# A modulation's columns: row sums of transposed weights on Vector in place of products on TensorE

## The chip, the core and the metric
One core of a Trainium2 chip runs one layer of a latent diffusion backbone. The metric is the time of one execution on the device in microseconds (us): the median of 3 runs, beside one execution that the hardware profiler recorded. The engines are PE (TensorE, matrix products), PEld (its weight loads), DVE (Vector), ACT (Scalar), POOL (GpSimd) and SP (SyncE, whose queue issues nearly all DMA transfers here).

## What is computed
One conditioning vector c gives six vectors of 2048 columns each: shift, scale and gate of the attention half, and shift, scale and gate of the feed-forward.

```python
mod = silu(c) @ ada_w + ada_b                      # ada_w: 2048 x 12288
sh1, sc1, g1, sh2, sc2, g2 = split(mod, 6)
z = modulate(rmsnorm(x, norm1_g), sh1, sc1) @ w_in # also for the context, with c_ctx
attn = windowed_gqa(...)                           # 16 heads, 4 kv heads, 512 tokens, 256 context tokens
rw = rwkv_output(...)                              # 16 heads of RWKV-7, both directions
x = x + g1 * (concatenate([attn, rw]) @ w_out)
x = x + g2 * swiglu(modulate(rmsnorm(x, norm2_g), sh2, sc2), w1, w3, w2)
return rmsnorm(x, final_norm_g)
```

There are 512 latent tokens, 256 context tokens, a width of 2048 and a feed-forward of 5632. All is float32. The last four of the six vectors are needed for the latents alone (the context isn't carried on after this layer), so they are one matrix-vector product with 8192 columns: 64 MB of weights, each used once.

## The kernel before
Channels lie on the 128 partitions and tokens along the row. Large products are made of three products of float32r parts (`mm3`, L109 to L114: high by high, low by high, high by low). A weight tile, 128x1024, is loaded into the ring `raw` (`split_weight`, L96 to L106, three buffers), Scalar copies its high part `whi` (L105) and Vector subtracts to get the low part `wlo` (L106). Of z = h @ w_in a column tile needs two such weights.

`modT` holds the modulation by columns of 128: 0 to 15 sh1, 16 to 31 sc1, 32 to 47 g1, 48 to 63 sh2, 64 to 79 sc2, 80 to 95 g2. `ada_group` (L146 to L171) computes 512 columns, that is four of these: eight loads of 512 KB (L154), 16 products 32x512 of silu(c) by the weights (L155, `ps_ada`), a copy to SBUF on Scalar (L164, `adas`), four small products that turn the row into columns (L167, `ps_adat`) and an addition of the bias on Vector (L168). Groups 0 to 7, sh1 and sc1, come at the start, before norm 1 can be finished. Groups 8 to 23 come as `ada_stream` (L1090) in the recurrence: its first loads wait for a load of w_out (`gate`), and its products are pinned where the program writes them.

The program then has these stages:
- **Start, keys and values**, to about 240 us: norms, the first groups of the modulation, the first column tiles of z. For the values four weights are split, and narrow products follow each.
- **Attention**, 240 to about 525 us. There are 32 units (2 groups by 4 blocks of queries by 4 pairs of heads). Of each: scores on TensorE, the row's maximum on Vector (L445), a few small steps (L447 to L449), Scalar's exponentials with their sum (L452), 1/sum and the scaling on Vector (L454 to L457), then transposes on TensorE (L466), their copy on Scalar (L467) and, every four units, the product by the values. Only TensorE's order is written by hand (`manual_schedule`): the scores of unit u + 2 go between the transposes of unit u, and shares of a stream of column tiles of z between both. The order of the other engines comes from a scheduler that simulates a timeline.
- **Preparation of the recurrence**, to about 1000 us.
- **Recurrence**, to about 1865 us: eight head pairs, each in three stretches of chunks, as streams `front`, inverse and chain (L860, L822, L967 and others). Behind each step's products `fill` lets other streams go on: `out_stream` (partial products of w_out, L110 to L114 under the name `ps_op`), `ada_stream` and `gate_stream`. How far each should be is a table, `DUE`. At the end of a pair stands `finish` with its output products (L994, `ps_y`).
- **Step to the feed-forward**: the last row tile of the recurrence's output is split (L1020, L1021, `alo`), the products with the last two row tiles of w_out go into the banks that are free, and `add_rows` (L1182) adds `g1` times them to x on Vector.
- **Feed-forward**, from about 1920 us: weights split as above (L1228 to L1231), 4 groups of 11 column tiles, `ps_u` and then `ps_d`, with `g2` at L1278.

Vector and SyncE execute in order: what waits holds back all that stands behind it on its engine.

## Time and profile before
| | |
|---|---|
| three runs | 3396.3, 3404.6, 3408.9 us; median 3404.6 |
| profiled execution | span 3398.9 us, 50708 instructions |
| busy share | PE 95%, DVE 49%, ACT 34%, POOL 17% |
| moved | 448 MB, 132 GB/s on the mean |

The profiled execution is one run of its own; its span is 5.7 us below the median of the runs. Busy time is the time in which an engine executes something. A wait is an engine's idle time just before an instruction, put down to what ended it. PEclk is the clock that TensorE was granted, as a share of its full speed of 2.4 GHz.

### The profile page before, as it was taken

The numbers are of one execution on the slowest core, as the hardware profiler recorded it, in microseconds if no ns is written. First come the engines' busy times: TensorE is split into PE (matmuls) and PEld (weight loads), VectorE is DVE, ScalarE is ACT, GpSimd is POOL, SyncE is SP. The second block draws the span as 40 slices with busy tenths as digits, with TensorE's granted clock in tenths as the row PEclk, the third lists the DMA queues.
The fourth block names the chain that finished last, engine by engine and source line by source line (L and its number), as shares of the span: only waits on it lengthen the run. The fifth ranks groups of instructions, "written<-read, shape, count | busy, mean of one in ns | idle before, by whom it ended". The sixth has DMA issues, their size and how long they took to land.

```text
span 3398.9 us, 50708 instructions
## 1 busy us (share of the span) xinstructions
PE 3238.6 (95%) x20448; PEld 2481.5 (73%) x20448; DVE 1652.3 (49%) x2674; ACT 1169.2 (34%) x2019; POOL 592.5 (17%) x613
## 2 busy tenths in 40 slices
PE   7899999889889999999998899999999999999997
PEld 3486667767665766777776688888888888888886
DVE  3345544786675666668876632332333332332333
ACT  4224443443434444445544422212221222212221
POOL 0000001563464423434442200000000000000011
PEclk9999999999989999999999899999999999999998
DMA  8611112333348789855557122322232223322232
GB/s 305 245 64 49 45 39 69 136 131 125 109 154 258 238 262 278 253 173 155 149 155 223 42 97 94 106 86 93 93 103 94 89 94 100 102 86 96 93 103 89
DMA packets 246858, 448.45 MB, mean 132 GB/s; under 512 B 84320, under 2 KB 131680, under 8 KB 246624
## 3 DMA queue, kind: packets, MB, share of 16 engines
q1 hardware_dynamic: 246624, 445.22, 40.6%
q8 instruction: 161, 2.64, 0.3%
q14 instruction: 73, 0.60, 0.1%
HBM read 383.52 MB, written 61.60 MB: 131 GB/s over the span
## 4 chain that ended last, share of the span: by engine, by line
PE 56%; DVE 3%; DMA 2%; ACT 1%; issue 1%; POOL 0%; SPq 0%; ACTq 0%; DVEq 0%; POOLq 0%
PE ps_u L114 10%; PE ps_u L113 10%; PE ps_u L110 9%; PE ps_d L110 5%; PE ps_d L114 5%; PE ps_d L113 5%; PE ps_m L941 2%; PE ps_y L822 1%; PE ps_op L110 1%; PE ps_i L860 1%; PE ps_x L811 1%; PE ps_w L930 1%; PE ps_op L113 1%; PE ps_op L114 1%; PE ps_ada L155 1%; PE ps_i L866 1%
## 5 line engine op out<-in xcount | busy, mean ns | idle before, releaser
L1230 ACT ACTIVATE whi<-raw 128x1024 fp32r<-128x1024 f32 (+1 forms) x240 | 275.1, 1147 | 1115.2 <-PE ps_u L113 585.6
L1231 DVE TENSOR_TENSOR wlo<-raw,whi 128x1024 fp32r<-128x1024 f32 (+1 forms) x238 | 317.8, 1336 | 557.3 <-ACT whi L1230 556.6
L114 PE MATMUL ps_u<-ahi,wlo 128*128 128x512 f32 x1408 | 560.8, 398 | 1.2 <-DVE wlo L1231 1.2
L113 PE MATMUL ps_u<-alo,whi 128*128 128x512 f32 x1408 | 557.9, 396 | 0.9 <-DVE alo L1246 0.9
L110 PE MATMUL ps_u<-ahi,whi 128*128 128x512 f32 x1408 | 553.3, 394 | 3.3 <-ACT ahi L1241 1.7
L110 PEld LDWEIGHTS ps_u<-ahi,whi 128*128 128x128 f32 x1408 | 265.1, 188 | 68.9 <-ACT whi L1230 2.9
L113 PEld LDWEIGHTS ps_u<-alo,whi 128*128 128x128 f32 x1408 | 265.2, 188 | 68.7 <-DVE alo L1246 1.6
L114 PEld LDWEIGHTS ps_u<-ahi,wlo 128*128 128x128 f32 x1408 | 265.1, 188 | 63.5 <-DVE wlo L1231 2.0
L198 POOL TENSOR_TENSOR sq<-sq 128x512 f32<-128x512 f32 x22 | 39.8, 1808 | 1429.4 <-ACT sq L194 1429.2
L113 PE MATMUL ps_d<-glo,whi 128*128 128x512 f32 x704 | 273.3, 389 | 0.0
L110 PE MATMUL ps_d<-ghi,whi 128*128 128x512 f32 x704 | 273.3, 389 | 0.0
L114 PE MATMUL ps_d<-ghi,wlo 128*128 128x512 f32 x704 | 273.3, 389 | 0.0
L114 PE MATMUL ps_z<-hhi,wlo 128*128 128x512 f32 x544 | 221.1, 406 | 38.9 <-DVE wlo L106 38.9
L110 PE MATMUL ps_z<-hhi,whi 128*128 128x512 f32 x544 | 228.1, 419 | 2.5 <-DVE wad L278 1.3
L113 PE MATMUL ps_z<-lo,whi 128*128 128x512 f32 x544 | 220.2, 405 | 0.0
L1278 DVE SCALAR_TENSOR_TENSOR x<-ps_d,modT,x 128x512 f32<-128x512 f32 x64 | 48.1, 751 | 299.8 <-PE ps_d L114 299.8
L852 POOL TENSOR_TENSOR bdB<-XY,mk 64x256 f16<-64x256 f32 x192 | 146.6, 764 | 266.0 <-DVE XY L813 248.2
L106 DVE TENSOR_TENSOR wlo<-raw,whi 128x1024 fp32r<-128x1024 f32 x80 | 123.0, 1544 | 137.7 <-ACT whi L105 134.5
L114 PEld LDWEIGHTS ps_z<-hhi,wlo 128*128 128x128 f32 x544 | 106.1, 195 | 69.6 <-DVE wlo L106 46.3
L155 PE MATMUL ps_ada<-ada,siluT 128*32 128x512 f32 x768 | 137.6, 612 | 18.1 <-DMA ada<-ada_w 14.1
L114 PEld LDWEIGHTS ps_d<-ghi,wlo 128*128 128x128 f32 x704 | 132.2, 188 | 27.5
L110 PEld LDWEIGHTS ps_d<-ghi,whi 128*128 128x128 f32 x704 | 132.2, 188 | 27.4
(617 smaller groups left out, 5824.3 us busy)
## 6 DMA issues: line engine op xcount, KB each, us to landing
ada<-ada_w SPq DMA_DIRECT2D x192, 512.0 KB, 6.0
raw<-w SPq DMA_DIRECT2D x176, 512.0 KB, 3.2
raw<-w SPq DMA_DIRECT2D x64, 704.0 KB, 4.1
raw<-w_in SPq DMA_DIRECT2D x72, 512.0 KB, 3.3
p1d<-pr SPq DMA_DIRECT2D x64, 256.0 KB, 3.2
bkd<-bk SPq DMA_DIRECT2D x16, 768.0 KB, 5.4
XB<-bkd SPq DMA_DIRECT2D x96, 128.0 KB, 3.9
pr<-p1d SPq DMA_DIRECT2D x48, 256.0 KB, 3.1
```

What stands on the lines that cost most here:

```text
L106: nc.vector.tensor_tensor(lo, raw, hi.bitcast(F32), op=ALU.subtract)
L110: mm = nc.tensor.matmul(ps, lhsT=whi, rhs=hhi, start=first, stop=False)
L113: nc.tensor.matmul(ps, lhsT=whi, rhs=hlo, start=False, stop=False)
L114: nc.tensor.matmul(ps, lhsT=wlo, rhs=hhi, start=False, stop=last)
L155: mm = nc.tensor.matmul(ps[32 * i:32 * i + 32, :], lhsT=siluT[:, 4 * q + i, :], rhs=a[:, i % 2, :], start=(q == 0), stop=(q == 3))
L198: eng.tensor_tensor(self.acc[eng], self.acc[eng], sq, op=ALU.add)
L811: nc.tensor.matmul(px[:, u, :], lhsT=AL[:, d, s_ + u, :], rhs=XB[:, d, s_ + u, :], start=True, stop=True)
L852: nc.gpsimd.tensor_tensor(diag(B[l], h, d), ab[h][:, d], lm(l, h, d), op=ALU.mult)
L941: nc.tensor.matmul(pm[m, u, :n], lhsT=WT[e][h][:, d, u, m], rhs=YB[h][:, d, u, :n], start=True, stop=True)
L1230: nc.scalar.activation(hi[:, :n], raw[:, :n], AF.Copy)
L1231: eng.tensor_tensor(lo[:, :n], raw[:, :n], hi[:, :n].bitcast(F32), op=ALU.subtract)
L1278: nc.vector.scalar_tensor_tensor(x1[:, j, :], ps, modT[:, 80 + j, 0:1], x1[:, j, :], op0=ALU.mult, op1=ALU.add)
```

## The change
Columns 32 to 95 of `modT` are no longer products. `ada_w` keeps its first eight groups; the other columns come transposed as `ada_t`, 64 column tiles x 2 halves x 128 columns x 1024 channels. So a column lies on a partition and its 2048 weights along the row. silu(c) is spread over all partitions once, at the start (`siluB`, 128x2048, by 16 products and four copies). A new generator `ada_rows` takes, for one column tile and one half, a load of 512 KB into a ring named `raw` and one instruction on Vector that multiplies the row by `siluB` and writes the sum to `macc`. After 16 column tiles two small additions on Vector put them into `modT` with the bias.

The generator is advanced at two places. From the ring of the projections' weights, 48 column tiles (g1, sh2, sc2; 96 rows): four rows ahead of each of the values' four weights, then two or three ahead of each attention unit. From the ring of the feed-forward's weights, 16 column tiles (g2; 32 rows): four ahead of each of the column tiles 1 to 8. Both rings get a fourth buffer. `ada_stream` with its entry in `DUE` and its gate are gone, and the ring `ada` in the recurrence, which now serves the gates' weights alone, is called `gu`, with two buffers.

```diff
-        raw = wp.tile([P, 1024], F32, tag="raw", name="raw", bufs=3)
+        raw = wp.tile([P, 1024], F32, tag="raw", name="raw", bufs=4)
...
+    def ada_rows(pool, tag, shape, bufs, cols):
+        for j in cols:
+            for h in range(2):
+                a = pool.tile(shape, F32, tag=tag, name="arow", bufs=bufs)[:, :1024]
+                nc.sync.dma_start(a, ada_t[j - 32, h])
+                nc.vector.scalar_tensor_tensor(a, a, 1.0, siluB[:, 1024 * h:1024 * h + 1024], op0=ALU.mult, op1=ALU.mult,
+                                               accum_out=macc[:, j - 32, h:h + 1])
+                yield
+            if j % 16 == 15:
+                c0 = j - 15
+                nc.vector.tensor_tensor(modT[:, c0:c0 + 16, 0], macc[:, c0 - 32:c0 - 16, 0], macc[:, c0 - 32:c0 - 16, 1],
+                                        op=ALU.add)
+                nc.vector.tensor_tensor(modT[:, c0:c0 + 16, 0], modT[:, c0:c0 + 16, 0], pc("adab", c0, 16), op=ALU.add)
...
+            for q in range(4):
+                pb = ps_mm.tile([P, 512], F32, tag="mm", name="ps_sb")
+                for i in range(4):
+                    nc.tensor.matmul(pb[:, i * P:(i + 1) * P], lhsT=siluT[:, 4 * q + i, 0:1].broadcast_to([P, P]), rhs=ident,
+                                     start=True, stop=True)
+                nc.scalar.copy(siluB[:, 512 * q:512 * q + 512], pb)
...
+            rows = ada_rows(wp, "raw", [P, 1024], 4, range(32, 80))
             for q in range(4):
+                advance(rows, 4)
...
+                    advance(rows, 3 if u % 2 else 2)
...
+                run(rows)
...
-        DUE = (((-1.5, 0), (17.0, 176), (18.8, 176), (22.0, 224)), ((-1.5, 0), (22, 128)), ((-3, 0), (-2, 16)))
+        DUE = (((-1.5, 0), (17.0, 176), (18.8, 176), (22.0, 224)), ((-3, 0), (-2, 16)))
...
-        def ada_stream():
-            for j in range(8, 24):
-                yield from ada_group(fr, ps_mm, "ma", siluT, sel, j, 2, 1, tc.keep_in_program_order,
-                                     gate[0] if j == 8 else None)
...
-            raw = wf.tile([P, WT], F32, tag="raw", name="raw", bufs=3)
+            raw = wf.tile([P, WT], F32, tag="raw", name="raw", bufs=4)
...
+        rows = ada_rows(wf, "raw", [P, WT], 4, range(80, 96))
...
+                if not first:
+                    advance(rows, 4)
```

Three places of the order show what moves; the numbers at a row's start are its place on the engine. Line numbers of the changed kernel differ: L463 is the softmax's maximum (L445 of before), L467 the last step ahead of the exponentials (L449), L472 the first step behind them (L454), L106 the weights' low part in both.

On Vector in the attention, before: a weight's low part, then one softmax after the other (the row with x2 at its end stands for two).

```order
283 L106 TENSOR_TENSOR wlo<-raw,whi 128x1024
284 L449 TENSOR_SCALAR sm<-sm 128x2
285 L454 TENSOR_TENSOR sm<-sm 128x2
286 L455 RECIPROCAL sm<-sm 128x2
287 L457 TENSOR_SCALAR pr<-pr,sm 128x512 x2
288 L445 TENSOR_REDUCE sm<-ps_s 128x2
289 L447 SCALAR_TENSOR_TENSOR sm<-sm,par 128x2
290 L448 TENSOR_TENSOR sm<-par,sm 128x2
291 L449 TENSOR_SCALAR sm<-sm 128x2
292 L454 TENSOR_TENSOR sm<-sm 128x2
```

The same on Vector after the change; L171 is a row's sum, `arow` its tile.

```order
430 L463 TENSOR_REDUCE sm<-ps_s 128x2
431 L171 SCALAR_TENSOR_TENSOR arow,macc<-arow,siluB 128x1024
432 L465 SCALAR_TENSOR_TENSOR sm<-sm,par 128x2
433 L171 SCALAR_TENSOR_TENSOR arow,macc<-arow,siluB 128x1024
434 L466 TENSOR_TENSOR sm<-par,sm 128x2
435 L467 TENSOR_SCALAR sm<-sm 128x2
436 L171 SCALAR_TENSOR_TENSOR arow,macc<-arow,siluB 128x1024
437 L472 TENSOR_TENSOR sm<-sm 128x2
438 L473 RECIPROCAL sm<-sm 128x2
439 L171 SCALAR_TENSOR_TENSOR arow,macc<-arow,siluB 128x1024
440 L475 TENSOR_SCALAR pr<-pr,sm 128x640 x2
441 L106 TENSOR_TENSOR wlo<-raw,whi 128x1024
```

Rows now stand between a softmax's steps, ahead of the exponentials as well as behind them.

On Vector at the step to the feed-forward, before: the last row tile's low part (L1021) and the additions.

```order
1947 L1015 SCALAR_TENSOR_TENSOR y<-y,par,bv 128x512
1948 L1016 TENSOR_TENSOR y<-y,gt 128x512
1949 L1021 TENSOR_TENSOR alo<-y,ahi 128x512
1950 L1182 SCALAR_TENSOR_TENSOR x_18804<-ps_o,modT,x_18804 128x512 x7
1951 L198 TENSOR_TENSOR sq<-sq 128x512
```

The same place after the change (L1040 is the low part, L1194 the additions):

```order
2019 L1034 SCALAR_TENSOR_TENSOR y<-y,par,bv 128x512
2020 L1035 TENSOR_TENSOR y<-y,gt 128x512
2021 L171 SCALAR_TENSOR_TENSOR arow,macc<-arow,siluB 128x1024
2022 L1040 TENSOR_TENSOR alo<-y,ahi 128x512
2023 L171 SCALAR_TENSOR_TENSOR arow,macc<-arow,siluB 128x1024 x2
2024 L1194 SCALAR_TENSOR_TENSOR x_18468<-ps_o,modT,x_18468 128x512 x2
2025 L171 SCALAR_TENSOR_TENSOR arow,macc<-arow,siluB 128x1024
2026 L1194 SCALAR_TENSOR_TENSOR x_18468<-ps_o,modT,x_18468 128x512 x6
```

The first four of the feed-forward's rows have come ahead of it, one before the low part and three among the additions.

On TensorE in the recurrence, before: the end of a pair's steps with four of the modulation's products.

```order
5918 L860 LDWEIGHTS bdQ_7080
5919 L860 MATMUL ps_i<-Zn,bdQ_7080 128x64
5920 L994 MATMUL ps_y<-y,cf 128x512
5921 L155 MATMUL ps_ada<-ada,siluT 32x512 x4
5922 L860 LDWEIGHTS bdP_7056
5923 L860 MATMUL ps_i<-Z_10951,bdP_7056 128x64
```

The same place after the change (L879 is L860 of before, L1013 is L994):

```order
5869 L879 LDWEIGHTS bdA_7392
5870 L879 MATMUL ps_i<-Tm,bdA_7392 128x64
5871 L1013 MATMUL ps_y<-y,cf 128x512
5872 L879 LDWEIGHTS bdP_7376
5873 L879 MATMUL ps_i<-Z_10869,bdP_7376 128x64
```

The modulation's products are gone from between the others.

## Rows read from the trace of the kernel before

**Rows 1.** The page, part 1: busy time, share of the span, instructions.
```profile
PE 3238.6 (95%) x20448; PEld 2481.5 (73%) x20448; DVE 1652.3 (49%) x2674; ACT 1169.2 (34%) x2019; POOL 592.5 (17%) x613
```

**Rows 2.** Windows: stretch, its length, busy time of each engine; clock, DMA share, GB/s.
```profile
core 0: us, PE busy (x) PEld busy (x) DVE busy (x) ACT busy (x) POOL busy (x), PEclk, DMA share, GB/s
170.00:238.50 68.50, 67.88 (x445) 61.96 (x443) 26.96 (x43) 11.86 (x16) 0.00 (x0) 1.00 0.21 72
238.50:489.00 250.50, 245.60 (x1167) 162.70 (x1167) 121.70 (x269) 107.14 (x238) 0.00 (x0) 0.99 0.13 43
1052.00:1100.00 48.00, 43.31 (x446) 25.90 (x440) 23.45 (x58) 18.80 (x44) 11.39 (x16) 1.00 0.91 280
1100.00:1203.20 103.20, 102.89 (x1212) 71.87 (x1211) 60.41 (x145) 50.65 (x118) 37.66 (x54) 1.00 0.77 240
1203.20:1315.40 112.20, 110.11 (x1284) 77.91 (x1281) 71.83 (x173) 55.36 (x129) 39.33 (x54) 1.00 0.89 264
1315.40:1426.20 110.80, 108.08 (x1260) 76.17 (x1257) 71.29 (x172) 49.64 (x117) 38.96 (x54) 1.00 0.87 266
1426.20:1530.10 103.90, 98.52 (x1178) 73.48 (x1174) 70.27 (x173) 49.68 (x118) 39.02 (x54) 1.00 0.62 184
1530.10:1619.00 88.90, 87.56 (x1103) 70.42 (x1104) 72.72 (x176) 47.70 (x115) 38.80 (x54) 1.00 0.53 155
1619.00:1701.20 82.20, 79.61 (x1076) 64.96 (x1071) 68.22 (x167) 46.49 (x114) 36.88 (x54) 1.00 0.51 146
1865.00:1895.00 30.00, 24.39 (x115) 20.27 (x116) 19.91 (x26) 12.04 (x19) 14.22 (x11) 0.83 0.11 36
1925.00:2100.00 175.00, 174.25 (x746) 139.62 (x745) 52.97 (x55) 40.98 (x47) 1.13 (x1) 1.00 0.28 93
```

**Rows 3.** The chain that ended last: start, length, the piece where two pairs part.
```profile
1315.55 0.94 PE ps_y L994 x2
```

**Rows 4.** Windows of line 155 alone: the modulation's products (PE and PEld).
```profile
1052.00:1100.00 48.00, 13.48 (x66) 1.84 (x60) 1.00 0.91 280
1100.00:1203.20 103.20, 20.74 (x128) 3.19 (x128) 1.00 0.77 240
1203.20:1530.10 326.90, 49.26 (x320) 7.34 (x320) 1.00 0.80 239
```

**Rows 5.** Windows of line 167 alone: the small transposing products.
```profile
1052.00:1100.00 48.00, 1.98 (x16) 2.02 (x16) 1.00 0.91 280
1100.00:1203.20 103.20, 2.93 (x24) 2.99 (x24) 1.00 0.77 240
1203.20:1530.10 326.90, 11.37 (x88) 11.15 (x88) 1.00 0.80 239
```

**Rows 6.** Windows of line 110 alone: first product of each output triplet, by pair.
```profile
1203.20:1315.40 112.20, 13.36 (x28) 5.27 (x28) 1.00 0.89 264
1530.10:1619.00 88.90, 14.35 (x30) 5.66 (x30) 1.00 0.53 155
1619.00:1701.20 82.20, 8.49 (x18) 3.39 (x18) 1.00 0.51 146
```

**Rows 7.** TensorE's waits, 1052 to 1530.1 us: total, times, longest.
```profile
PE ps_ada L155 <- DMA ada<-ada_w: 6.2, 8, 1.4
PE ps_ada L155 <- DVE Tm L880: 2.4, 1, 2.4
```

**Rows 8.** Three lines' instructions: shortest/median/longest in ns, first and last start, forms.
```profile
L106 DVE TENSOR_TENSOR wlo<-raw,whi x80: 1209/1226/2644, 36.2 to 991.6; 128x1024 fp32r<-128x1024 f32 x80
...
L662 DVE SCALAR_TENSOR_TENSOR ta<-ta,kk x16: 957/1451/2490, 589.5 to 994.2; 128x768 f32<-128x768 f32 x16
...
L452 ACT ACTIVATION_READ_ACCUMULATOR pr<-ps_s,sm x64: 189/198/209, 243.5 to 520.9; 128x1 f32 x64
```

**Rows 9.** Vector's waits, 238.5 to 489 us.
```profile
DVE sm L445 <- PE ps_s L435: 57.5, 20, 7.8
DVE sm L454 <- ACT pr L452: 40.9, 25, 2.3
```

**Rows 10.** DMA issues, 280 to 520 us: count, KB each, median us to landing.
```profile
raw<-w_in SPq DMA_DIRECT2D x15, 512.0 KB, 3.3
```

**Rows 11.** Timeline of Vector at the step to the feed-forward: start, length.
```profile
1875.97 4.47 DVE L1182 SCALAR_TENSOR_TENSOR x<-ps_o,modT,x 128x512 f32<-128x512 f32 x6 [2.72 <-PE ps_o L114]
```

**Rows 12.** Timeline of Scalar at the start: its first work on x.
```profile
14.63 0.63 ACT L333 ACTIVATE sq<-x__171 128x512 f32<-128x512 f32 x1 [9.10 <-DMA x__171<-xT]
```

More of the change, by code (lines that the diff above doesn't have):

```diff
@@ L63, in hybrid_layer_kernel @@
 @with_exitstack
-def hybrid_layer_kernel(ctx: ExitStack, tc: tile.TileContext, xT, ctxT, pcol, ada_w, w_in, lora_up, w_out, w13, w2,
+def hybrid_layer_kernel(ctx: ExitStack, tc: tile.TileContext, xT, ctxT, pcol, ada_w, ada_t, w_in, lora_up, w_out, w13, w2,
                         c_f32, c_rwkv, c_rope, c_mask, out):
@@ L144, in rsqrt_tokens, with ada_group @@
         return y
-    def ada_group(pool, psp, pstag, siluT, sel, j, nbuf=2, psbuf=2, pin=None, behind=None):
+    def ada_group(pool, psp, pstag, siluT, sel, j, nbuf=2, psbuf=2):
         ps = psp.tile([P, 512], F32, tag=pstag, name="ps_ada", bufs=psbuf)
@@ L152, in ada_group @@
                     a = pool.tile([P, 2, 512], F32, tag="ada", name="ada", bufs=2 * nbuf)
-                    with tc.issue_after(behind) if behind and q < nbuf else nullcontext():
-                        nc.sync.dma_start(a, ada_w[j, q, :, i:i + 2, :])
-                mm = nc.tensor.matmul(ps[32 * i:32 * i + 32, :], lhsT=siluT[:, 4 * q + i, :], rhs=a[:, i % 2, :],
-                                      start=(q == 0), stop=(q == 3))
-                if pin and i % 4 == 0:
-                    pin(mm)
-                if pin and i % 4 == 4 - 1:
-                    yield True
-            if not pin:
-                yield
+                    nc.sync.dma_start(a, ada_w[j, q, :, i:i + 2, :])
+                nc.tensor.matmul(ps[32 * i:32 * i + 32, :], lhsT=siluT[:, 4 * q + i, :], rhs=a[:, i % 2, :],
+                                 start=(q == 0), stop=(q == 3))
         ad = pool.tile([P, 512], F32, tag="adas", name="adas", bufs=1)
@@ L169, in ada_group @@
                                 pc("adab", 4 * j, 4).unsqueeze(2).broadcast_to([P, 4, 2]), op=ALU.add)
-        if not pin:
-            yield
+    def ada_rows(pool, tag, shape, bufs, cols):
[11 more added lines that the diff above has]
+                nc.vector.tensor_tensor(modT[:, c0:c0 + 16, 0], modT[:, c0:c0 + 16, 0], pc("adab", c0, 16), op=ALU.add)
     class MeanSquare:
@@ L222, in hybrid_layer_kernel @@
     sel = const.tile([P, 2], F32, name="sel")
+    siluB = const.tile([P, D], F32, name="siluB")
+    macc = const.tile([P, 64, 2], F32, name="macc")
     ysx = ExitStack()
@@ L728, in hybrid_layer_kernel @@
         XB = fr.tile([P, 2, H, 192], F32, name="XB")
-        gu = [fr.tile([P, 2, 512], F32, tag="ada", name="gu", bufs=4) for _ in range(2)]
+        gu = [fr.tile([P, 2, 512], F32, tag="gu", name="gu", bufs=2) for _ in range(2)]
         with tc.high_priority():
@@ L762, in fill @@
             at_ = stretch + min(1.0, own_ns / 17000)
-            due = [0, 0, 0]
+            due = [0, 0]
             for e, pts in enumerate(DUE):
@@ L772, in fill @@
                 some = False
-                for e, st in enumerate((st_o, st_a, st_g)):
+                for e, st in enumerate((st_o, st_g)):
                     if n_done[e] < int(due[e]) and next(st, False):
@@ L1334, in host_layout @@
                                 col(a0), col(k_k), col(k_a), col(r_k), col(lnx_g), col(lnx_b), sink, cc], 1)
-    a["ada_w"] = ada_w[0].reshape(4, 4, P, 24, 512).transpose(3, 0, 2, 1, 4)
+    a["ada_w"] = ada_w[0].reshape(4, 4, P, 24, 512)[:, :, :, :8].transpose(3, 0, 2, 1, 4)
+    a["ada_t"] = ada_w[0][:, 4096:].T.reshape(64, P, 2, 1024).transpose(0, 2, 1, 3)
     gu = np.zeros((256, 1024), f)
```

13 lines of the change are left out of this document (6 added, 7 removed).

## The prediction, made before the changed kernel ran
> **What bounds the kernel now.** I read the page's busy lines first, then the windows (busy time of each engine by stretch), then the same windows for the two lines that go, then waits and single lines. TensorE is busy 95% of the span [rows 1], so what is taken from it can count, but only where the stretch itself waits for it. The windows show five such stretches [rows 2]. In the weights' and first scores' stretch (170 to 238.5 us) and in the attention (238.5 to 489) TensorE is busy 67.9 of 68.5 and 245.6 of 250.5 us, Vector 27.0 and 121.7, the DMA share is 0.21 and 0.13. In the recurrence, head pair by head pair (the 1315.4 that parts two of them is a pair's first output product on the chain of waits, [rows 3]), TensorE is busy 110.1 of 112.2 us, 108.1 of 110.8, 98.5 of 103.9, and then, with no modulation left, 87.6 of 88.9 and 79.6 of 82.2. Vector has 68 to 73 us of work in every one of these pairs. So in both places TensorE sets the pace, Vector is half idle in the attention, and less idle in the recurrence.
>
> **What leaves the recurrence.** 256 products and their small transposing products, with 128 loads of 512 KB. Busy time of the two lines in [rows 4, 5]: 13.48 + 1.98 = 15.5 us from 1052 to 1100, 20.74 + 2.93 = 23.7 from 1100 to 1203, 49.26 + 11.37 = 60.6 in the three full pairs to 1530.
> - Three pairs. Does the time come back? The profile has the answer in itself: the pair from 1530 runs without these products and takes 88.9 us with 30 triplets of the output projection, the next 82.2 with 18 [rows 6], so 0.56 us a triplet. A pair with 28 or 29 triplets should take some 88 us: 112.2 + 110.8 + 103.9 = 326.9 now, 263 to 264 then, 63 less. By busy time it is 60.6, and 8.6 us of waits go with it (6.2 for their loads, 2.4 of the product behind another engine, [rows 7]). I take 64.
> - The ramp, 1100 to 1203, has TensorE busy 102.9 of 103.2: 22 of the 23.7.
> - 1052 to 1100: TensorE is busy 43.3 of 48 and the DMA share is 0.91, so part of it only fills waits: 0 to 15.5, I take 8, and the loads that leave can make it more.
> Sum: **-94 us** (bounds -80 and -110). What is late next is TensorE's own work, as from 1530 on; Vector's 72 of some 88 us is close, but it is no later than in the pair from 1530.
>
> **What the rows cost.** A row is one load of 512 KB and one Vector instruction, 128x1024, two float32 sources in SBUF, with a sum. No row of before shows Vector with an accumulator. Nearest: the plain 128x1024 instruction takes 1.226 us, and the same kind of instruction (two SBUF float32 sources, 128x768) 957 ns at least, which is the same slope [rows 8]. Scalar's accumulating exps are followed by a read of the accumulator of 198 ns [rows 8]. So 1.23 to 1.43 us a row; below 1.23 nothing speaks for it. I take 1.33: 128 rows are 170 us of Vector. On a second instruction for the sum the Trainium skill agrees with the row on Scalar ("VectorE: DVE Perf Modes", section "Two Vector instructions with no wait between them": an operation that writes its accumulator counts as two instructions).
> By the new order 25 rows stand ahead of the first softmax maximum, 71 in the attention, 4 at the step to the feed-forward, 28 in its first eight tiles.
> - Ahead of the scores (170 to 238.5): 27.0 + 25 x 1.33 = 60 of 68.5 us on Vector fit. Their loads are 13.1 MB beside 4.9 (72 GB/s), 18 MB, 75 us at the 240 GB/s that [rows 2] shows from 1100 on, 64 at the 280 before that. The values' weights stand behind rows in SyncE's queue. 0 to +15, I take **+5**.
> - Attention. Vector waits 57.5 us for scores and 40.9 for Scalar's exps [rows 9]. It works in order: a wait is cover only if a row stands in it. 18 of the 32 softmaxes have a row between the maximum and the wait for the exps; the other 14 keep theirs, 40.9 x 14/32 = 18 us. Then the landings: the row's tile shares four buffers with the weights' pairs. 19 of the rows use the buffer that the row just ahead has freed, and a load takes 3.3 us [rows 10]: 3.3 + 1.33 = 4.6 us a row, where 2.5 rows per unit of 7.8 us leave 3.1. That is 1.5 us late for each, 29 us; the rest alternate two buffers (2.3 us a row) and are in time. Vector's need: 121.7 + 71 x 1.33 + 18 + 29 = 263 against 250.5, +12. With 1.43 and twice the landings it is 298, +48; if the waits for scores take in the landings, 0. What Vector is late with are probabilities that TensorE transposes, so it falls on the path, less the two units that scores run ahead. I take half way, **+25**.
> - Step to the feed-forward (1865 to 1895, TensorE 24.4 of 30): one row stands ahead of the last row tile's low part, two more ahead of the first addition of the residual, where before the additions start at 1875.97 [rows 11]. The third and fourth load only once a buffer is free, which holds back all that is queued behind them: additions, so banks. 1.3 (one row) to 12 (four rows and two loads), I take **+6**.
> - Feed-forward: 28 x 1.33 = 37 us on a Vector with 53 of 175 busy, DMA share 0.28 [rows 2]; a weight's low part stands behind two rows at most. 0 to 10, **+4**.
> - Start: 16 products and four copies for the spread vector. Scalar idles for 9.1 us until the first row of x lands at 14.63 [rows 12]; nothing is late while that cover holds, else four copies at the 0.63 of that row, 2.5 us. **0**. So are the eight small additions into the modulation: 16 columns each, in stretches where Vector idles.
>
> Sum: -94 + 5 + 25 + 6 + 4 = -54. The profiled execution has a span of 3398.9 us, 5.7 below the median of the runs: 3398.9 - 54 + 5.7 = **3350 us**.
>
> **Rivals.**
> 1. *The rows lie wholly in Vector's waits.* For it: 98 us of waits there against 94 us of rows, and TensorE runs two units ahead. Against: the order puts rows where they stand, and four buffers for two users make loads follow each other. Attention 0, the step +3: -94 + 0 + 5 + 3 + 2 = -84, **3320 us**. Chance 0.12.
> 2. *Slower: the summing instruction runs at half the rate.* Its place is the attention; its price 2.45 us a row instead of 1.33. Then Vector needs 121.7 + 71 x 2.45 + 18 + 29 = 343 of 250.5 us, +92; ahead of the scores 27 + 61 = 88 of 68.5, +20; the step +10, feed-forward +4: +126 - 94 = +32, **3437 us**. The added Vector time grows by 100 us per us of row length, and it eats the gain from about 2.1 us a row (71d + 25d + 4d - 119 = 94). Against it: two float32 sources without a sum run at full rate [rows 8]. For it: nothing here shows them with one. The Trainium skill has this as a rule ("Vector Engine (DVE) Microarchitecture Reference", section "7. Points that are easy to get wrong": a scalar_tensor_tensor with two sources in SBUF that are not bf16 runs at half throughput, both read ports being taken and none left to read the accumulator back). By that rule the 128x768 instruction of [rows 8] would be twice as long as it is, so the trace disagrees for the form without a sum, and I give it 0.11.
> 3. *The recurrence gives back only half.* If the products filled waits of the chain of head pairs, taking them out leaves waits. For it: the first stretch, 1052 to 1100, does that, and Vector has 70 of 88 us of work. Against: the pair from 1530. Then -47 + 40 = -7, **3398 us**. Chance 0.10.
> The change does what it says in the order of the engines: no modulation product stands in TensorE's row after the first eight groups, and nothing else there has moved; no rival is made of that.
>
> **How the numbers follow.** Forecast 0.67, own range 3308 to 3392; rivals 0.12, 0.11, 0.10. The predicted time is the forecast's, 3350. All the low bounds together give 3296, all the high ones 3411, but they don't come together. From 3305 to 3400 the range holds the forecast nearly whole, the first rival and most of the third; the slower one is left out, about 0.19 in all. A measurement of this kernel can tell about 0.5%, 17 us, from no change. Faster by more than that (under 3387): most of the forecast 0.64, rival 1 0.12: 0.76 less a little for the bounds, 0.75. Within: 0.14 (rival 3 and the forecast's upper end). Slower: 0.11 (rival 2).
>
> **What would show it.** The length of one row (1.2 to 1.45 us, against 2.45); pairs of the recurrence of 86 to 89 us from 1203's successor on, all alike but for triplets (rival 3: over 98); the attention's stretch 20 to 30 us longer, with Vector waiting for row loads and TensorE for probabilities (rival 1: as long as now); the step to the feed-forward some 6 us longer with rows ahead of the low part. It would be wrong if the row's loads took far longer than 3.3 us in each other's company, so that Vector stands behind SyncE's queue through the whole attention: at 6 us each the 19 rows alone would be 80 us late. It would also be wrong if preparation, which the change leaves in place, came out in another order with other waits.

## The result, and the profile after

The changed kernel takes 3353.26 us (median of 4 runs, 3342.86 to 3359.73), the kernel before 3402.64 (median of 4 runs, 3396.3 to 3408.87): a ratio of 0.9855, 95% interval 0.9837 to 0.9872. The forecast was 3350 us, 54 us less than before; it is 49 less. The profiled execution has a span of 3349.2 us against 3398.9. But the sum came out for partly wrong reasons, and that is what the rest is about.

Page, part 1, of the changed kernel (answers to [rows 1]):

```profile
PE 3176.8 (95%) x19840; PEld 2478.9 (74%) x19840; DVE 1796.6 (54%) x2922; ACT 1160.7 (35%) x2007; POOL 593.1 (18%) x613
```

TensorE has 608 products fewer, but only 62 us less of busy time, although the products that left the recurrence were busy for some 100 us [rows 4, 5]. Vector has 144 us more. So other products took longer.

To see where, I cut both traces at the same instructions: the first score of the attention, its last transpose, the last product of the preparation, the first and the last output product of a head pair. Windows of the kernel before, then of the changed one, each in three stretches: attention (first score to last transpose), the recurrence ahead of the first pair's output, the pairs.

```profile
238.50:525.10 286.60, 279.97 (x1359) 187.31 (x1358) 137.59 (x307) 123.71 (x274) 0.00 (x0) 0.99 0.13 42
1005.30:1203.20 197.90, 182.31 (x1876) 119.40 (x1874) 112.25 (x250) 86.78 (x200) 85.36 (x126) 0.97 0.84 251
1203.20:1854.70 651.50, 622.86 (x7532) 474.66 (x7529) 468.20 (x1125) 322.38 (x763) 240.96 (x332) 0.99 0.68 202
```

```profile
227.40:567.90 340.50, 302.87 (x1357) 200.61 (x1357) 222.75 (x467) 122.14 (x274) 0.00 (x0) 0.91 0.48 156
1047.80:1210.00 162.20, 148.46 (x1663) 113.54 (x1662) 113.02 (x249) 83.98 (x199) 85.95 (x127) 0.95 0.51 145
1210.00:1800.80 590.80, 568.00 (x7104) 459.64 (x7101) 463.64 (x1110) 315.84 (x751) 240.24 (x332) 0.98 0.53 154
```

| stretch | forecast | measured |
|---|---|---|
| start, to the first score | 0, and +5 for the values' rows | 238.5 to 227.4: -11.1 |
| attention | +25 (0 to 48) | 286.6 to 340.5: +53.9 |
| preparation | 0 | -0.3 |
| recurrence ahead of the first pair's output | -30 | 197.9 to 162.2: -35.7 |
| pairs | -64 | 651.5 to 590.8: -60.7 |
| step to the feed-forward | +6 | 38.6 to 40.9: +2.3 |
| feed-forward | +4 | 1505.6 to 1507.5: +1.9 |
| sum | -54 | -49.7 |

The attention's row shows the surprise: the same products (1357 of 1359 recorded) are busy 302.9 us instead of 280.0, at a granted clock of 0.91 instead of 0.99. So of its 53.9 us, 31.0 are idle time of TensorE (6.6 to 37.6) and 22.9 are products at a lower clock. Windows of 10 us in the changed kernel's attention show where:

```profile
240.00:250.00 10.00, 2.71 (x8) 1.97 (x9) 8.09 (x23) 3.73 (x11) 0.00 (x0) 0.50 0.72 244
250.00:260.00 10.00, 10.00 (x28) 6.92 (x28) 5.32 (x9) 1.81 (x4) 0.00 (x0) 0.50 0.50 160
...
280.00:290.00 10.00, 10.00 (x48) 5.31 (x47) 8.03 (x18) 5.15 (x13) 0.00 (x0) 1.00 0.61 180
...
320.00:330.00 10.00, 10.00 (x28) 7.03 (x28) 6.75 (x14) 2.35 (x7) 0.00 (x0) 0.50 0.53 191
```

TensorE is full from 250 to 260 and yet gets through 28 products, where the window from 280 holds 48 at the full clock: it runs at 0.50, that is 1.2 of 2.4 GHz, behind a wait. The waits stand in the timeline of TensorE, in brackets behind the product that ended them; the second is the one ahead of the window from 320:

```profile
247.29 1.12 PE L484 MATMUL ps_pt<-cf,pr 128*128 128x128 f32 x4 [11.48 <-DVE pr L475]
...
319.03 1.08 PE L484 MATMUL ps_pt<-cf,pr 128*128 128x128 f32 x4 [2.34 <-DVE pr L475]
```

So 0.50 stands behind a wait of 11.48 us and behind one of 2.34 us. The length of the last wait alone does not set it: behind 3.75 us that end at 447.14 the window from 450 to 460 has 0.77, behind 1.40 us that end at 300.49 the clock is full.

The waits of Vector and of TensorE in that attention (total, times, longest) answer to [rows 9] and [rows 7]:

```profile
DVE arow L171 <- DMA arow<-ada_t: 53.0, 46, 4.6
DVE sm L472 <- ACT pr L470: 28.0, 16, 2.5
DVE sm L463 <- PE ps_s L453: 22.0, 13, 3.8
```

```profile
PE ps_pt L484 <- DVE pr L475: 19.5, 4, 11.5
```

Vector now waits for rows to land, 53 us, and TensorE's largest wait is for probabilities. The row itself is as short as hoped (answers to [rows 8]):

```profile
L171 DVE SCALAR_TENSOR_TENSOR arow<-arow,siluB x128: 1206/1225/1228, 175.6 to 2029.8; 128x1024 f32<-128x1024 f32 x128
L171 DVE DVE_READ_ACCUMULATOR arow<-arow,siluB x128: 74/83/86, 176.8 to 2031.0; 128x1 f32 x128
```

1.225 + 0.083 = 1.31 us. At the step to the feed-forward (answers to [rows 11]) a row of 1.22 us stands ahead of the low part, and three behind it, ahead of and among the additions, one of them behind a wait for its load:

```profile
1818.99 1.22 DVE L171 SCALAR_TENSOR_TENSOR arow<-arow,siluB 128x1024 f32<-128x1024 f32 x1
...
1823.89 1.23 DVE L171 SCALAR_TENSOR_TENSOR arow<-arow,siluB 128x1024 f32<-128x1024 f32 x1 [1.93 <-DMA arow<-ada_t]
```

### The profile page after: what moved, and what is told of

It is laid out like the page before. It is cut to its first block, busy times and chain, and to the rows that moved or that the text cites. A ratio compares the mean times of both kernels' runs of the same rounds, so it can differ in the third digit from the quotient of the medians.

```text
span 3349.2 us, 49778 instructions
## 1 busy us (share of the span) xinstructions
PE 3176.8 (95%) x19840; PEld 2478.9 (74%) x19840; DVE 1796.6 (54%) x2922; ACT 1160.7 (35%) x2007; POOL 593.1 (18%) x613
## 4 chain that ended last, share of the span: by engine, by line
PE 59%; DVE 4%; DMA 1%; issue 1%; POOL 1%; ACT 1%; SPq 0%; DVEq 0%; ACTq 0%; POOLq 0%
PE ps_u L114 10%; PE ps_u L113 10%; PE ps_u L110 10%; PE ps_d L113 5%; PE ps_d L110 5%; PE ps_d L114 5%; PE ps_m L960 2%; PE ps_x L830 2%; PE ps_op L110 2%; PE ps_y L841 2%; PE ps_i L879 1%; PE ps_w L949 1%; PE ps_op L114 1%; PE ps_op L113 1%; PE ps_c L986 1%; PE ps_i L885 1%
## 5 line engine op out<-in xcount | busy, mean ns | idle before, releaser
L205 POOL TENSOR_TENSOR sq<-sq 128x512 f32<-128x512 f32 x22 | 40.9, 1860 | 1432.8 <-ACT sq L201 1432.5
L171 DVE SCALAR_TENSOR_TENSOR arow<-arow,siluB 128x1024 f32<-128x1024 f32 x128 | 156.4, 1223 | 111.5 <-DMA arow<-ada_t 110.8
L106 DVE TENSOR_TENSOR wlo<-raw,whi 128x1024 fp32r<-128x1024 f32 x80 | 122.9, 1543 | 83.4 <-ACT whi L105 82.2
L113 PEld LDWEIGHTS ps_d<-glo,whi 128*128 128x128 f32 x704 | 132.1, 188 | 27.5
```

The source lines that it names most:

```text
L106: nc.vector.tensor_tensor(lo, raw, hi.bitcast(F32), op=ALU.subtract)
L113: nc.tensor.matmul(ps, lhsT=whi, rhs=hlo, start=False, stop=False)
L171: nc.vector.scalar_tensor_tensor(a, a, 1.0, siluB[:, 1024 * h:1024 * h + 1024], op0=ALU.mult, op1=ALU.mult, accum_out=macc[:, j - 32, h:h ...
```

## The experiments

Questions: is the recurrence's gain all of what the products took there; and what makes the attention longer: Vector's work, the landing of the rows, or the place at which a row stands?

The expectations measure the attention from the first softmax maximum to the last: 276.3 us before, 321.9 in the changed kernel. That yardstick is too short by what the first maximum itself stands behind rows (10.9 us after the first score, 2.5 before), so the results below also give first score to last transpose: 286.6 and 340.5.

### 1. The modulation left out of the recurrence

```diff
-        st_i, st_o, st_a, st_g = [], out_stream(), ada_stream(), gate_stream()
+        st_i, st_o, st_a, st_g = [], out_stream(), iter(()), gate_stream()
+    nc.gpsimd.memset(modT[:, 32:, :], 0.0)
```

> The kernel before with the modulation's stream left out of the recurrence, nothing in its place (the modulation from column 32 on is zero). Prices what the recurrence gives back when nothing else changes. From the two traces the recurrence gave back 97 us (first to last output product of the pairs 60.7, ahead of them 36.5). If products and loads there are the whole cause: 95 to 99 us less than before, 3300 to 3308. If part of the 36.5 ahead of the first pair comes from elsewhere (buffers of the gates' weights, the DMA scratch): 10 us less of a gain, about 3315.

3296.14 us in its one run, 4 us below the range; span 3294.0. Windows: attention, recurrence ahead of the first pair's output, pairs.

```profile
230.80:517.30 286.50, 279.89 (x1357) 187.25 (x1357) 137.55 (x307) 123.83 (x274) 0.00 (x0) 0.99 0.13 42
997.10:1159.70 162.60, 148.91 (x1664) 113.51 (x1662) 112.42 (x249) 83.72 (x197) 85.69 (x126) 0.94 0.51 144
1159.70:1749.40 589.70, 564.39 (x7104) 455.94 (x7100) 462.98 (x1110) 316.17 (x751) 241.28 (x332) 0.99 0.52 154
```

The recurrence gives back 35.3 + 61.8 = 97.1 us, as in the changed kernel (96.4). The span falls by 104.9, mostly since this execution also reaches its first score at 230.8 us instead of 238.5 with the same program up to there, bar one fill of the modulation on GpSimd. So the start differs by some 8 us from one execution to another, and most of the changed kernel's -11.1 can be that. Whether a part of it is the change's own is open: among the kernels with row sums the first score lies between 226 and 247 us.

### 2. Work without loads, loads without work, a fifth buffer

```diff
-                nc.sync.dma_start(a, ada_t[j - 32, h])
-                nc.vector.scalar_tensor_tensor(a, a, 1.0, siluB[:, 1024 * h:1024 * h + 1024], op0=ALU.mult, op1=ALU.mult,
+                nc.vector.scalar_tensor_tensor(siluB[:, :1024], siluB[:, :1024], 1.0, siluB[:, 1024:], op0=ALU.mult, op1=ALU.add,
```

> The changed kernel without the 128 row loads: each row's Vector instruction stays, 128x1024 with a sum, but reads the spread vector that is already there (the modulation from column 32 on is wrong). Prices Vector's work alone. Theory A (landings): the attention comes back to 276 to 290 us, the whole to 3305 to 3318. Theory B (Vector's work and its place): the attention stays at 305 to 322, the whole at 3333 to 3350. Both: the recurrence's pairs as in the changed kernel.

```diff
-                nc.vector.scalar_tensor_tensor(a, a, 1.0, siluB[:, 1024 * h:1024 * h + 1024], op0=ALU.mult, op1=ALU.mult,
+                nc.vector.scalar_tensor_tensor(a[:, :16], a[:, :16], 1.0, siluB[:, 1024 * h:1024 * h + 16], op0=ALU.mult, op1=ALU.mult,
```

> The changed kernel with all row loads, but each row's Vector instruction reads 16 of the 1024 columns (the modulation from column 32 on is wrong). Prices the loads and the waits for them alone. Theory A (landings): the attention stays 10 to 35 us longer than the 276.3 before, since Vector still stands behind each load. Theory B (Vector's work): the attention is within 8 us of 276.3, the whole at 3305 to 3315.

```diff
-        raw = wp.tile([P, 1024], F32, tag="raw", name="raw", bufs=4)
+        raw = wp.tile([P, 1024], F32, tag="raw", name="raw", bufs=5)
...
-            rows = ada_rows(wp, "raw", [P, 1024], 4, range(32, 80))
+            rows = ada_rows(wp, "raw", [P, 1024], 5, range(32, 80))
```

> The changed kernel with five buffers instead of four in the ring that the projections' weights and the attention's rows share. To make room, only half of silu(c) is spread and used for both halves of a row, so the second halves of the modulation's sums are wrong; the instructions keep their size. In the changed kernel the attention, from the first softmax maximum to the last, takes 321.9 us against 276.3 before, and Vector waits 53.0 us there for rows to land (46 times). Theory A (landings set the lengthening: rows wait for a buffer and a load of 4.0 us): a fifth buffer takes at least a third of the waits away, the attention falls to 290 to 310, the whole to 3320 to 3340. Theory B (Vector's work itself and its place between softmax steps): waits fall a little, the attention stays within 6 us of 321.9, the whole at 3345 to 3355.

Windows of the attention, first without loads, then with the loads alone and with five buffers, each of these two followed by Vector's wait for rows in it (total, times, longest).

```profile
241.00:544.50 303.50, 288.71 (x1357) 193.06 (x1357) 161.89 (x357) 123.75 (x274) 0.00 (x0) 0.96 0.12 40
```

```profile
230.70:544.80 314.10, 287.95 (x1358) 190.96 (x1358) 147.86 (x465) 123.17 (x274) 0.00 (x0) 0.96 0.52 168
```

```profile
DVE arow L171 <- DMA arow<-ada_t: 86.0, 63, 4.3
```

```profile
237.10:575.30 338.20, 302.89 (x1359) 199.64 (x1358) 218.05 (x457) 123.72 (x274) 0.00 (x0) 0.91 0.46 151
```

```profile
DVE arow L171 <- DMA arow<-ada_t: 61.4, 49, 5.1
```

| | maximum to maximum | score to transpose | one run's time |
|---|---|---|---|
| before | 276.3 | 286.6 | |
| no loads (most rows ahead of the attention) | 292.3 (+16.0) | 303.5 (+16.9) | 3322.10 |
| loads, with 16 columns of work | 296.4 (+20.1) | 314.1 (+27.5) | 3320.51 |
| both (the changed kernel) | 321.9 (+45.6) | 340.5 (+53.9) | |
| both, five buffers | 321.1 (+44.8) | 338.2 (+51.6) | 3359.09 |

Neither theory held alone. The run without loads does not price what it was meant to price. Where no load holds a row back, the scheduler moved the rows forward: 106 of all 128, the feed-forward's among them, stand ahead of the first maximum, and the last one starts at 289.8 us. Windows of the rows' line in it, to the first score and in the attention (two instructions a row):

```profile
0.00:241.00 241.00, 128.85 (x210) 0.96 0.62 216
241.00:544.50 303.50, 28.21 (x48) 0.96 0.12 40
```

So its +16.9 us come with some 24 rows at the head of the attention, not with 71 spread over it. What Vector's work alone costs there no run here shows; the expectations below that take 16.0 or 292.3 us for it rest on this run.

The loads alone, with rows at nearly the places of the changed kernel, lengthen the attention as theory A said. But theory A's other half fell: a fifth buffer shortens nothing, and the waits for rows get no shorter. With five buffers the scheduler puts the rows still earlier in Vector's order: 28 stand ahead of the first maximum instead of 25, 47 ahead of the eighth instead of 41, 92 ahead of the 24th instead of 86. That this is why the buffer does not help is argued; no run has five buffers and a held order.

### 3. The same rows, at fixed places in Vector's order

A row is held behind all that the program has given to Vector ahead of it; one row of each unit stands between its exponentials and the step that waits for them, one or two behind its scaling.

```diff
-                    advance(rows, 3 if u % 2 else 2)
...
+                advance(rows, 1)
                 nc.vector.tensor_tensor(den, den, es, op=ALU.add)
...
                     nc.vector.tensor_scalar(pr[e][:, :n], pr[e][:, :n], den[:, e:e + 1], None, op0=ALU.mult)
+                advance(rows, 2 if u % 2 else 1)
...
+                if 40 <= j < 80:
+                    tc.keep_in_program_order(ins)
```

> The changed kernel with the attention's rows held at fixed places of Vector's order: one row of each unit between its exponentials and the step that waits for them, one or two behind its scaling; the rows ahead of the values and in the feed-forward as before. Loads, buffers and Vector's work are those of the changed kernel; only the place of a row, and so how long its load has had to land, differs. Without loads the attention was 16.0 us longer than before, without Vector's work 20.1, with both 45.6. Theory C (rows stand in Vector's order where their load has not landed and hold the softmax back): waits for rows fall from 53.0 us to under 25, the attention to 285 to 300, the whole to 3322 to 3337. Theory D (the loads cost by themselves, through the queue or the DMA engines, wherever the rows stand): the attention stays above 310, the whole above 3340.

3323.81 us (median of 4 runs), ratio to the kernel before 0.9784, interval 0.9768 to 0.9799. Window of the attention and TensorE's longest wait there:

```profile
236.30:552.80 316.50, 290.64 (x1359) 192.76 (x1358) 228.94 (x471) 125.81 (x275) 0.00 (x0) 0.95 0.51 169
```

```profile
PE ps_z L110 <- ACT whi L105: 17.2, 5, 8.9
```

307.2 by the first yardstick, 316.5 by the second: 24 us of the 53.9 are gone, with the same instructions and loads. What differs is the rows' place in Vector's order, and with it when their loads are issued: 16 rows instead of 25 stand ahead of the first maximum. A wait for a row's load no longer shows on Vector there. The attention itself missed the range of theory C (285 to 300), because a new wait took over: TensorE waits for high parts of weights that come late.

The next kernel only holds the rows where the changed kernel's program has them, two or three together ahead of each unit's part of the program:

```diff
+                if 40 <= j < 80:
+                    tc.keep_in_program_order(ins)
```

> The changed kernel with the attention's rows held two or three together behind the scaling of the unit before, none between a softmax's steps. Theory C: most of the gain of the fixed places stays, the attention 288 to 305; the waits for the exponentials, 28.0 us in the changed kernel, go back to the 41 of before. If the place between the steps is what matters (cover for the exponentials): no better than the changed kernel's 321.9.

```profile
227.60:563.30 335.70, 295.59 (x1359) 194.77 (x1358) 224.05 (x466) 123.40 (x274) 0.00 (x0) 0.92 0.46 153
```

```profile
PE ps_z L110 <- ACT whi L105: 26.9, 7, 9.1
```

323.2 and 335.7 us, 3348.94 in its one run: hardly better than the changed kernel, and outside theory C's range. Held together behind the scaling, rows don't make TensorE wait for probabilities any more (4.4 us), but the weights are later still (26.9), and the exponentials have less cover (Vector waits 37.7 us for them, instead of 28.0 in the changed kernel and 17.8 at the fixed places). So two things can count: a row in the wait for the exponentials, and how long a row holds the buffer that a weight needs. Section 6 tests the second.

### 4. A third of the rows to GpSimd and Scalar

```diff
+                if j < 80 and (2 * j + h) % 3 == 2:
+                    nc.gpsimd.tensor_tensor(a, a, siluB[:, 1024 * h:1024 * h + 1024], op=ALU.mult)
+                    nc.scalar.activation(a, a, AF.Copy, accum_out=macc[:, j - 32, h:h + 1])
```

> The changed kernel with a third of the 96 rows of projections and attention multiplied on GpSimd (a product 128x1024 took 2.3 us there) and summed on Scalar, both with time to spare in the attention. Loads and buffers as in the changed kernel; a buffer is held longer. Vector has 42 us less to do. Theory B (Vector's work and its place): the attention falls to 295 to 312. Theory D (loads by themselves): it stays within 6 us of 321.9, or gets longer by the later buffers.

316.3 by the first yardstick, 330.1 by the second; 3344.16 in its one run. Rows on GpSimd (line, count, busy, mean ns), the rows left on Vector, and the attention's window:

```profile
L172 POOL TENSOR_TENSOR arow<-arow,siluB 128x1024 f32<-128x1024 f32 x32 | 77.0, 2406 | 435.7 <-DMA arow<-ada_t 365.2 <-DVE sm L472 13.6 <-DVE sm L468 12.7
```

```profile
L176 DVE SCALAR_TENSOR_TENSOR arow<-arow,siluB x96: 1203/1225/2310, 177.8 to 2022.6; 128x1024 f32<-128x1024 f32 x96
```

```profile
236.10:566.20 330.10, 299.24 (x1357) 198.02 (x1358) 218.76 (x413) 149.43 (x325) 60.01 (x25) 0.94 0.47 159
```

Just at theory D's edge (5.6 us of the 6 it allowed), and 10 us shorter by the longer yardstick (340.5 to 330.1). But Vector did not get the 42 us that were taken from it. With 27 rows fewer in the attention (50 instead of 77) it is busy 218.8 us there, 4.0 less than in the changed kernel, since other instructions are longer, the softmax's small steps above all. One of them in the changed kernel, then in this one (count, busy, mean ns):

```profile
L465 DVE SCALAR_TENSOR_TENSOR sm<-sm,par 128x2 f32<-128x2 f32 x32 | 5.0, 156 | 0.2
```

```profile
L470 DVE SCALAR_TENSOR_TENSOR sm<-sm,par 128x2 f32<-128x2 f32 x32 | 14.2, 443 | 0.3
```

So this run does not part theories B and D: how much of the lengthening is the amount of Vector's work stays open.

### 5. The feed-forward's rows held as well

```diff
-                if 40 <= j < 80:
+                if j >= 40:
```

> As the kernel with fixed places, and the feed-forward's 32 rows are held behind what the program has issued to Vector ahead of them as well, so none stands at the step to the feed-forward. That step, from the last output product to the last residual, takes 40.9 us in the changed kernel and 38.6 before. If the rows there cost it: back to 38.6 (2 us), the whole 2 to 3 us below the kernel with fixed places in the attention alone. If not: the same within 1 us.

A clear miss: 3404.73 us (median of 10 runs), ratio 1.0028, interval 1.0017 to 1.0038. The step did get shorter, 36.1 us against 40.9. But what the rows there cost is not clear of the spread: without rows it takes 36.1, 38.6 (before) and 39.8 us (section 1), with rows 40.9, 43.2 (section 3) and 39.6 (section 7). And from the last addition of the residual to the first of the feed-forward it takes 357.9 us instead of 275.8. TensorE's wait from 1860 to 2120 us, and SyncE's timeline (start, length, issues):

```profile
PE ps_u L110 <- ACT whi L1245: 55.8, 7, 8.1
```

```profile
1883.62 3.76 SPq L1243 DMA_DIRECT2D raw<-w  x4
1889.58 15.20 SPq L170 DMA_DIRECT2D arow<-ada_t  x4
1916.79 3.76 SPq L1243 DMA_DIRECT2D raw<-w  x4
1922.57 15.71 SPq L170 DMA_DIRECT2D arow<-ada_t  x4
```

Weights and rows take turns: four weights, four rows, and the next weights come 27 us after the group of rows began. By the program, a held row stands behind the column tile's last work on Vector and keeps its buffer until then, and the next tile's weights need that buffer; the order of the queue fits this, and no run tests it here.

### 6. Buffer or queue

With the rows at fixed places, late weights have two possible causes: the shared ring of four buffers, which are handed out in turn, and SyncE's queue, in which a weight's load stands behind loads that wait for a buffer. Three kernels part them. In all of them the rows ahead of the values are held too, which they are not in section 3, so the three are best compared with each other. Two rings:

```diff
-        raw = wp.tile([P, 1024], F32, tag="raw", name="raw", bufs=4)
+        raw = wp.tile([P, 1024], F32, tag="raw", name="raw", bufs=2)
...
-            rows = ada_rows(wp, "raw", [P, 1024], 4, range(32, 80))
+            rows = ada_rows(wp, "arow", [P, 1024], 2, range(32, 80))
```

> Rows at fixed places (those ahead of the values held too), and the four buffers parted: two for the weights, two for the rows; all loads still on SyncE's queue. With fixed places and one shared ring the rows' waits were gone, but TensorE waited 17.2 us for weights' high parts that came late, and the attention was 307.2 us, 30.9 over the kernel before. Theory E (a weight waits for the row that holds its buffer): these waits fall under 5 us, the attention to 285 to 298. Theory F (a weight's load stands behind row loads in SyncE's queue, which wait for a buffer): they stay above 10 us, the attention at 300 to 312.

The other queue, with two rings and with one:

```diff
-                nc.sync.dma_start(a, ada_t[j - 32, h])
+                (nc.gpsimd if j < 80 else nc.sync).dma_start(a, ada_t[j - 32, h])
```

> As the kernel with two rings, and the rows of projections and attention are issued by GpSimd, which is idle there, instead of SyncE. Theories E and F: the weights' waits are gone, the attention at 285 to 297 us (Vector's work alone made it 292.3), the whole at 3308 to 3322. If it stays above 303, the transfers themselves are what delays the weights.

> Rows at fixed places with the one shared ring of four, and the rows' loads issued by GpSimd. Theory F (SyncE's queue): as good as with two rings and GpSimd, the attention at 285 to 297. Theory E (the shared buffers): still late weights, the attention at 300 to 312, the whole at 3320 to 3332.

Window of the attention, then waits in it: two rings (TensorE's longest, Vector's for rows); two rings and the other queue (Vector's for rows); the other queue alone (TensorE's longest).

```profile
227.30:532.80 305.50, 285.72 (x1357) 190.35 (x1357) 232.79 (x481) 123.83 (x274) 0.00 (x0) 0.97 0.56 184
```

```profile
PE ps_pt L488 <- DVE pr L478: 9.1, 1, 9.1
...
DVE arow L171 <- DMA arow<-ada_t: 16.1, 20, 1.9
```

```profile
229.70:540.90 311.20, 289.02 (x1358) 192.43 (x1358) 233.27 (x480) 123.83 (x274) 44.72 (x83) 0.96 0.54 180
```

```profile
DVE arow L171 <- DMA arow<-ada_t: 25.1, 23, 2.6
```

```profile
247.10:565.90 318.80, 291.10 (x1358) 193.16 (x1358) 229.24 (x473) 125.70 (x275) 40.55 (x76) 0.95 0.51 168
```

```profile
PE ps_z L110 <- ACT whi L105: 17.5, 5, 8.8
```

| | maximum to maximum | score to transpose | wait for weights | time |
|---|---|---|---|---|
| one ring, SyncE (section 3) | 307.2 | 316.5 | 17.2 | 3323.81 |
| two rings, SyncE | 285.5 | 305.5 | none listed | 3312.75 (one run) |
| two rings, GpSimd | 298.6 | 311.2 | none listed | 3314.47, ratio 0.9755 (0.9738 to 0.9771) |
| one ring, GpSimd | 308.6 | 318.8 | 17.5 | 3341.62, ratio 0.9837 (0.9822 to 0.9852) |

Theory E: the buffer. The last two kernels differ in the rings alone, and the wait for weights is there with one ring only; with one ring the queue makes no difference to it (17.2 and 17.5). Two rings of two are better than one of four. With GpSimd issuing, two rings missed their range by 1.6 us by the first yardstick: GpSimd, idle there otherwise, is busy 44.7 us with the issues, and Vector waits longer for rows, 25.1 us instead of 16.1; why is open. The last kernel missed its range for the whole (3320 to 3332) by 10 us. That is not the attention's alone: its values' products took 41.9 us instead of 34.2, and its first score came at 247.1 us.

### 7. Fewer rows ahead of the first softmax

```diff
-                advance(rows, 4)
+                advance(rows, 3)
...
-                advance(rows, 2 if u % 2 else 1)
+                advance(rows, 0 if u < 2 else 2 if u % 2 or u % 4 == 0 else 1)
```

> As the kernel with two rings and all loads on SyncE's queue, with fewer rows ahead of the first softmax: three instead of four ahead of each of the values' weights, none behind the scaling of the first two units, the rest given to later units. There, in the kernel with two rings, the first scores start at 227.3 us but the first maximum at 239.6, behind rows, TensorE waits 9.1 us for the first probabilities and runs at half its clock until about 257. From the first score to the last transpose it takes 305.5 us, the kernel before 286.6. Theory G (the rows at the head cost that wait and the slow stretch behind it): the wait falls under 3 us, the stretch to 288 to 297, the whole to 3298 to 3310. If the later units have no room for these rows: 300 or more, the whole at 3310 to 3320.

3306.75 us (median of 5 runs), ratio to the kernel before 0.9733, interval 0.9715 to 0.9751: the fastest version here, 46 us below the changed kernel by the medians. Window of the attention, TensorE's and Vector's waits:

```profile
225.70:526.70 301.00, 286.74 (x1357) 191.69 (x1357) 232.68 (x482) 123.91 (x274) 0.00 (x0) 0.97 0.57 187
```

```profile
PE ps_pt L488 <- DVE pr L478: 1.8, 1, 1.8
...
DVE arow L171 <- DMA arow<-ada_t: 16.3, 19, 2.4
```

The wait for the first probabilities is 1.8 us instead of 9.1, as theory G said, and the whole is in its range; the stretch from first score to last transpose is 301.0, 4.5 us shorter, and just in the range of the other theory: part of what the head gave up, the later units took. From the first maximum to the last it is 290.7 us, 5.2 longer than with two rings and more rows at the head. The rows' cost in the attention is now 14.4 us (286.6 to 301.0): 7.6 us more idle time of TensorE, and 6.8 us more of the same products at a clock of 0.97 instead of 0.99. The whole is 10.6 us above the kernel of section 1, which computes no modulation from column 32 on (one run).

## Why the prediction was right, and where it wasn't

**The recurrence** (-94). Right, and for its reason: -96.4 in the changed kernel, -97.1 with the modulation's stream left out of the kernel before. The comparison with the pair that had no modulation gave -64 for the pairs, and they gave 60.7 and 61.8. The three full pairs take 87.4, 88.1 and 89.2 us in the changed kernel, 264.7 together, where 263 to 264 were forecast. The stretch ahead of them gave more than the 30 of the forecast, 35.7: the share from 1052 to 1100 was halved there, and the text allowed that the loads that leave can make it more. Rival 3 is out.

**The row** (1.33 us, 1.23 to 1.43). Right: 1.31. Rival 2, half rate with a sum, is out at 1.225 us for the instruction itself. The Trainium skill's rule in "Vector Engine (DVE) Microarchitecture Reference", section "7. Points that are easy to get wrong", would have it at twice that; the trace disagrees, with the sum as without it. The Trainium skill's other statement, in "VectorE: DVE Perf Modes", section "Two Vector instructions with no wait between them", agrees: the sum's read is an instruction of its own, 83 ns.

**The attention** (+25, 0 to 48). Wrong in size, and outside its bounds: +53.9. Three steps of the term failed.

The first is its base, "121.7 + 71 x 1.33 + 18 + 29 = 263 against 250.5". The stretch to 489 us holds 28 of the 32 softmax maxima, but all 71 rows and all 32 softmaxes were set against it. Line 445 of the kernel before, in that stretch and behind it, and Vector's waits for exponentials over the whole attention:

```profile
238.50:489.00 250.50, 38.53 (x28) 0.99 0.13 43
489.00:525.10 36.10, 4.89 (x4) 1.00 0.11 37
```

```profile
DVE sm L454 <- ACT pr L452: 48.8, 29, 2.5
```

Over the whole attention Vector is busy 137.6 of 286.6 us, and the same sum is 137.6 + 94.4 + 48.8 x 14/32 + 29 = 282 us, less than the stretch. By its own rule the term was 0. TensorE's additional idle time was 31.0 us, near the 25, and that is luck.

The second is the landings: 29 us for 19 rows, measured 53.0 in 46 waits, with loads that took 4.0 us there in the median instead of 3.3. More buffers were not the remedy: a fifth brought nothing, the place in Vector's order (with the load times that follow from it) brought 24 us, and parting the buffers, with the values' rows held too, 11 more.

The third is "What Vector is late with ... falls on the path", costed as idle time of TensorE alone. Behind such waits TensorE was granted half its clock for a while: 22.9 us more for the same products (279.97 to 302.87 at clocks of 0.99 and 0.91). A row of this kind was in the trace of before: 0.83 where TensorE was busy 24.4 of 30 us [rows 2].

**Ahead of the scores** (+5). The values' products took 34.2 us in both, so nothing there; the delay came out later, as the first wait of the attention: the first maximum stood 10.9 us behind the first score instead of 2.5, and 11.48 us of TensorE's waiting followed. The term belonged to the attention; with fewer rows at the head, 12 instead of 16 ahead of the first maximum, that wait fell from 9.1 to 1.8 us in section 7.

**The step and the feed-forward** (+6, +4). +2.3 and +1.9, both in their bounds. The step's 2.3 us are not clear of its spread between kernels without rows there (36.1 to 39.8).

**The start** (0). -11.1 in these two executions. Two executions of a program that is the same up to there, bar one fill, differ by 7.7, so most of it can be that, and it was not forecast. It covers more than a third of what the attention was over.

So the sum was right by cancelling: the attention 29 us over its term, the start 11 under, the values' rows 5, the step and the feed-forward 6, the recurrence 2. The range, 3305 to 3400, held it with room; the forecast's confidence in the attention's bounds was not earned. Rival 1, rows wholly in Vector's waits at 3320 us, was not what this order gave. With the places held, the buffers parted and fewer rows at the head, the whole is at 3306.75, below it; but the rows still cost the attention 14 us there, where rival 1 had none, and the first score comes 12.8 us sooner than before. One sum is off by a little: the high bounds of the terms give 3410, not 3411.

## What to carry to other kernels

Side work on an engine that executes in order costs what it stands in front of, not only what it is busy for: it belongs where the engine waits anyway, behind a load that has long landed, and the place has to be held if the scheduler would pull it ahead. Loads that are used at once and loads that lie waiting for a slot should not take turns in one ring of buffers: with the rows held, two rings of two were better than one of four. A stall of TensorE has to be costed twice where the granted clock falls behind it, as the wait and as the slower products (31.0 and 22.9 us here). A stretch of a trace has to hold as many units as the sum counts that is set against it. And a kernel that leaves something out to price the rest also frees the scheduler: see where the rest went before its time is read as a price.

## What was not expected of the hardware

- A wait of 11.48 us of TensorE was followed by 0.50 of its clock from 247 to 260 us, one of 2.34 us by 0.50 from 320 to 330 us; over the whole attention that came to 22.9 us beside 31.0 us of waits.
- Vector's sum along the row is nearly free: 83 ns beside 1225, and two float32 sources in SBUF run at the same rate as the plain subtraction of [rows 8].
- A multiplication 128x1024 on GpSimd took 2.41 us, and in that kernel some of Vector's rows took up to 2.31 us instead of at most 1.23, and a softmax step 128x2 took 443 ns in the mean instead of 156.
- The start ends at 230.8 and 238.5 us in two executions of code that is the same up to there, bar one fill on GpSimd.
